# 1/rms of the query heads: four instructions of GpSimd, one per block of 128 tokens, in place of one for all four

## The chip, the cores and the metric

The kernel runs on one core of a Trainium2 chip. Five engines work on their own queues, each in order: TensorE (PE; its weight loads are listed as PEld), VectorE (DVE), ScalarE (ACT), GpSimd (POOL) and SyncE (SP), which here issues nearly all DMAs. They wait for each other through semaphores. The metric is the device time of one execution in microseconds (us), the median of several runs.

## What is computed

A transformer-like encoder layer on two sequences of 512 tokens and 1024 channels: a half-step feed-forward network, a mixing block (grouped-query attention beside an mLSTM memory), and a second half-step feed-forward network. The change touches the attention's queries. Their projection is split into 8 heads of 64, each head is divided by its root mean square, scaled by a gain, and rotated:

```
def rms_norm(x, g):
    xf = x.astype(jnp.float32)
    y = xf * lax.rsqrt(jnp.mean(xf * xf, axis=-1, keepdims=True) + EPS)
    return (y * g.astype(jnp.float32)).astype(x.dtype)
...
    h = rms_norm(x, mix_norm)
    proj = h @ w_in
...
    aq = apply_rope(rms_norm(aq.reshape(B, S, ATT_HEADS, ATT_HEAD_DIM), q_norm), cos, sin)
    ak = apply_rope(rms_norm(ak.reshape(B, S, ATT_KV_HEADS, ATT_HEAD_DIM), k_norm), cos, sin)
    av = av.reshape(B, S, ATT_KV_HEADS, ATT_HEAD_DIM)
    att = gqa_block_attention(aq, ak, av)
```

For a token there are 8 such numbers, one per head; for the 512 tokens, as 4 blocks of 128 on the partitions, a tile of 128 x 32.

## The kernel before

The program goes through the first feed-forward network for both sequences together, then the mixing of sequence 0, the mixing of sequence 1 (begun while the output projection of sequence 0 is still under way), and the second feed-forward network. Matmuls run in fp32 split into a high and a low part (three matmuls for one product), so TensorE is the engine with by far the most work.

In the mixing of a sequence, `mix` first projects keys, values and gate inputs (`kv_done`), then the queries (`q_done`), with tokens on the partitions: four PSUM banks, one per block of 128 tokens. From there:

- `q_done` works through the four blocks. ScalarE copies a block out of PSUM (L811), squares it (L758, in `sumsq`), and VectorE sums the squares of each head (L759) into 8 columns of the tile `ssq`, which has 32 columns.
- When all four blocks are summed, `rstd_cols` (L161 to L168) adds a small constant (L165) and takes the power -0.5 (L167), both on GpSimd, for all 32 columns at once.
- `q_rope(b)` rotates block `b`: `rope_apply` multiplies by the 1/rms (L770) and by the tables (L774, L779) and adds (L781), on VectorE. Then the result is split into a high and a low part (L631 on ScalarE, L632 on VectorE), TensorE transposes it, four heads at a time (L915), and ScalarE copies it to `qT` (L916). The scores of the attention (L975) read `qT`.

Between them stand, in the same stretch, the gates of the memory (L856 to L865), the turning of the keys (`k_turn`, L821 and L823), and the projections of the memory's queries and keys (L729 on TensorE, L892 on VectorE, weights through L213 and L214). A framework's scheduler fixes each engine's order at build time, by priorities; at run time every queue is in order. `small(w, tag)` gives a tile of `w` columns, two buffers for each tag; `rstd_cols` takes its result from a pool with four buffers for each width.

Of the kernel before, what the change touches and what calls it, by code (L numbers as in the profile page):

```python
# [26 lines left out]
def encoder(ctx, tc, I, outs):  # L27
# [14 lines left out]
    def nm(s):  # L42
        n_id[0] += 1
        return f"{s}_{n_id[0]}"

    @contextmanager
    def shifted(n):

        tc.cur_priority += n
        yield  # L50
        tc.cur_priority -= n
# [8 lines left out]
    def T2(dtype=F32, tag="t2"):  # L60
        if tag in ("eb", "ac"):
            i = boxes[tag]
            boxes[tag] += 1
            return boxes["tile"][:, i % 4 + (4 if tag == "ac" else 0), :]
        if tag == "R":
            return spool.tile([P, S], dtype, tag="R", bufs=2, name=nm("R"))
        n = {"t2": 11, "f2": 4}[tag]
        return tpool.tile([P, S], dtype, tag=tag, bufs=n, name=nm(tag))
# [47 lines left out]
    def PT():  # L116
        return pt.tile([P, S], F32, tag="t", name=nm("pst"))

    def f(ap):
        return ap.bitcast(F32)  # L120
# [40 lines left out]
    def rstd_cols(v, width, eps=EPS):  # L161

        a = spool.tile([P, width], F32, tag=f"rs{width}", bufs=4, name=nm("rs"))
        if eps:
            nc.gpsimd.tensor_scalar(a, v, eps, None, op0=ALU.add)  # L165
            v = a
        nc.gpsimd.tensor_tensor(a, v, nhalf[:, 0:width], op=ALU.pow)  # L167
        return a  # L168
# [460 lines left out]
    def split(src, hi, lo, eng=None):  # L629

        nc.scalar.activation(hi, src, AF.Copy)  # L631
        (eng or V_).tensor_tensor(lo, src, f(hi), op=ALU.subtract)  # L632


    HA, HK, DA = 8, 2, 64
# [3 lines left out]
    def small(w, tag):  # L639
        return spool.tile([P, w], F32, tag=tag, bufs=2 if tag != "asm" else 6, name=nm(tag))  # L640
# [4 lines left out]
    tabs = []  # L645
# [88 lines left out]
    def mix(s, xh, xl, early=None, extra=None, after=None):  # L734
# [21 lines left out]
        def sumsq(t, to):  # L756
            q2 = T2()
            nc.scalar.activation(q2, t, AF.Square, scale=DA ** -0.5)  # L758
            V_.tensor_reduce(to, q2.rearrange("p (h e) -> p h e", e=DA), axis=AX.X, op=ALU.add)  # L759

        def rope_apply(t, rq, tab, bsel):

            cg, sg = tab
            if bsel is None:
                nb, cb, sb = 4, cg.unsqueeze(2).to_broadcast([P, 4, 2, DA]), sg
            else:
                nb, cb, sb = 1, cg[:, bsel].unsqueeze(1).to_broadcast([P, 8, DA]).unsqueeze(1), sg[:, bsel:bsel + 1]
            hn_ = 8 // nb
            n = T2()
            V_.tensor_tensor(n.rearrange("p (h e) -> p h e", e=DA), t.rearrange("p (h e) -> p h e", e=DA),  # L770
                             rq.unsqueeze(2).to_broadcast([P, 8, DA]), op=ALU.mult)
            o, m = T2(), T2()
            v4 = lambda x: x.rearrange("p (b h e) -> p b h e", b=nb, e=DA)
            V_.tensor_tensor(v4(o), v4(n), cb, op=ALU.mult)  # L774
            v5 = lambda x: x.rearrange("p (b h i two) -> p b h i two", b=nb, h=hn_, two=2)
            s4 = sb.rearrange("p b (i two) -> p b i two", two=2)
            for bb in range(nb):
                for e in range(2):
                    V_.tensor_tensor(v5(m)[:, bb, :, :, e], v5(n)[:, bb, :, :, 1 - e],  # L779
                                     s4[:, bb, :, e].unsqueeze(1).to_broadcast([P, hn_, DA // 2]), op=ALU.mult)  # L780
            V_.tensor_tensor(o, o, m, op=ALU.add)  # L781
            return o
# [22 lines left out]
        qraw, rq = [], []  # L805

        def q_done(pq):
            ssq = small(32, "ssq")
            for b in range(4):
                t = T2()  # L810
                nc.scalar.activation(t, pq[b], AF.Copy, scale=r[s][:, b:b + 1])  # L811
                sumsq(t, ssq[:, b * 8:(b + 1) * 8])
                qraw.append(t)
            rq.append(rstd_cols(ssq, 32))

        def k_turn():
            for hk in range(HK):
# [87 lines left out]
            return win_cols(2320 + h * P, done)  # L905

        def q_rope(b):
            qo = rope_apply(qraw[b], rq[0][:, b * 8:(b + 1) * 8], tabs[0], b).rearrange("p (h e) -> p h e", e=DA)
            for g in range(2):
                qs = T2(F32R).rearrange("p (h u e) -> p h u e", u=2, e=DA)  # L910
                split(qo[:, g * 4:g * 4 + 4], qs[:, :, 0, :], qs[:, :, 1, :])
                with shifted(60):
                    p = PT()
                    for h in range(4):
                        nc.tensor.transpose(p[:, h * P:(h + 1) * P], f(qs[:, h]).rearrange("p u e -> p (u e)"), ident)  # L915
                    nc.scalar.activation(qT[:, g * 4:g * 4 + 4, b * P:(b + 1) * P],  # L916
                                         p.rearrange("p (h t) -> p h t", t=P), AF.Copy)

        go(*tok_proj(xh, xl, [(512, 256), (2304, 16)], 2, kv_done))
        if early:  # L920
            early()
        go(*tok_proj(xh, xl, [(0, 512)], 2, q_done), mem_qk(0, 0))
        yield None
        gates()
        k_turn()
        for b in range(4):
            q_rope(b)
# [281 lines left out]
    def turn(s, k, bank):  # L1209
        p = bank()  # L1210
        for b in range(4):
            nc.tensor.transpose(p[:, b * P:(b + 1) * P], raws[s][:, b, k * P:(k + 1) * P], ident)
        return p
# [58 lines left out]
    for k in range(HK_):  # L1272
        x1l, x1u = x1[2 * k % 4], x1[(2 * k + 1) % 4]
        for t, kk, bank, kr in ((x1l, k, PS, orow[3]), (x1u, k + HK_, PT, orow[4])):
            p = turn(1, kk, bank)
# [220 lines left out]
```

## Time and profile before

| | |
|---|---|
| median of 3 runs | 2094.67 us (2092.39 to 2095.3) |
| span of the profiled execution | 2089.2 us (from its first to its last instruction; the profile gives no time of its own beyond it) |
| PE busy | 2062.1 us, 99% |
| DVE busy | 1537.8 us, 74% |
| ACT busy | 896.4 us, 43% |
| POOL busy | 137.8 us, 7% |
| mixing of sequence 0: queries summed, 1/rms taken | 690 to 701 us |
| mixing of sequence 1: the same | 1041 to 1052 us |

How to read the rows: "L759" is line 759 of the kernel, "ssq<-t" says what is written from what, "128x8" is partitions by elements. A row of the timeline has start, duration, engine, line and operation, and in brackets how long the engine had been idle and what ended that. A row of the groups has count, busy time in us, mean ns of one instruction, and the idle time before it. A row of one line's instructions has minimum, median and maximum in ns. A row of the waits has the total in us, the number of times, and the longest. Matmuls are pipelined, so that their shown durations overlap; their rhythm is the distance of their starts.

### The profile page before, as it was taken

The page shows a single profiled execution, that of the slowest core. Times are in us where ns is not written, and L with a number is a line of the kernel's source. Part 1 is how long each engine was busy: PE and PEld are TensorE (multiplying, and loading weights), DVE is VectorE, ACT ScalarE, POOL GpSimd, SP SyncE. Part 2 cuts the span into 40 slices and gives each one's busy share as a digit, 9 for nine tenths or more (in the row PEclk, how much of TensorE's full clock was granted, in tenths as well). Part 3 has the DMA queues.
Part 4 walks back from the last instruction along what each step waited for, and adds up shares of the span by engine and source line. Part 5 has one row for each costly group of instructions (what it writes and reads, how often), then busy time and mean ns, then how long its engine had stood idle before and what let it go on. Part 6 is the DMA issues. An engine that isn't in the chain of part 4 may idle for free.

```text
span 2089.2 us, 27103 instructions
## 1 busy us (share of the span) xinstructions
PE 2062.1 (99%) x9488; PEld 1696.6 (81%) x9488; DVE 1537.8 (74%) x2612; ACT 896.4 (43%) x1645; POOL 137.8 (7%) x145
## 2 busy tenths in 40 slices
PE   8999999999999999999999999999999999999998
PEld 6888888888888777888887788888888888888887
DVE  6888988786796698574557845445888888795796
ACT  7544444442235466463444543323544444442222
POOL 1000000001004112110220000001000000000010
PEclk9999999999999999999999999999999999999999
DMA  9655655699766646778776345677656555599753
GB/s 286 198 178 185 202 171 178 207 347 355 264 221 234 194 149 209 252 241 278 224 252 211 121 152 182 204 251 244 205 169 216 184 179 182 180 342 351 273 189 116
DMA packets 304185, 458.52 MB, mean 219 GB/s; under 512 B 20304, under 2 KB 170848, under 8 KB 303024
## 3 DMA queue, kind: packets, MB, share of 16 engines
q1 hardware_dynamic: 303456, 455.52, 65.2%
q0 software_dynamic: 592, 1.27, 0.3%
q8 instruction: 75, 1.23, 0.2%
q14 instruction: 62, 0.51, 0.1%
HBM read 289.82 MB, written 166.89 MB: 219 GB/s over the span
## 4 chain that ended last, share of the span: by engine, by line
PE 93%; DVE 2%; DMA 1%; ACT 1%; issue 1%; POOL 1%; SPq 0%; DVEq 0%; POOLq 0%; ACTq 0%
PE mm L729 18%; PE pss L307 17%; PE pst L307 11%; PE mm L307 11%; PE mm L563 8%; PE pst L563 4%; PE pss L563 4%; PE mm L713 4%; PE pso L563 3%; PE pso L1002 1%; PE pso L713 1%; PE pss L975 1%; PE pst L994 1%; PE pso L1141 1%; PE pss L729 1%; PE pst L729 1%
## 5 line engine op out<-in xcount | busy, mean ns | idle before, releaser
L729 PE MATMUL mm<-xh,w 128*128 128x512 f32 x896 | 292.3, 395 | 0.4 <-DMA w<-wpark 0.4
L307 PE MATMUL pss<-xc,w 128*128 128x512 f32 x1056 | 256.4, 392 | 0.0
L307 PE MATMUL mm<-xc,w 128*128 128x512 f32 x1056 | 252.9, 391 | 3.6 <-ACT w L265 1.6
L307 PE MATMUL pst<-xc,w 128*128 128x512 f32 x1056 | 253.7, 389 | 0.0
L307 PEld LDWEIGHTS pss<-xc,w 128*128 128x128 f32 x1056 | 197.0, 188 | 47.2 <-DVE t L338 6.6
L307 PEld LDWEIGHTS mm<-xc,w 128*128 128x128 f32 x1056 | 197.5, 188 | 46.0 <-ACT w L265 2.5
L307 PEld LDWEIGHTS pst<-xc,w 128*128 128x128 f32 x1056 | 198.3, 188 | 41.2
L729 PEld LDWEIGHTS mm<-xh,w 128*128 128x128 f32 x896 | 168.3, 189 | 34.5 <-DMA w<-wpark 0.8
L563 PE MATMUL mm<-rt,w 128*128 128x512 f32 (+1 forms) x819 | 189.1, 385 | 0.0
L729 PE MATMUL mm<-xl,w 128*128 128x512 f32 x448 | 177.0, 395 | 0.0
L563 PEld LDWEIGHTS mm<-rt,w 128*128 128x128 f32 x819 | 151.7, 188 | 29.9
L265 ACT ACTIVATE w<-t 128x512 fp32r<-128x512 f32 x176 | 107.0, 627 | 138.3 <-issue 55.2
L266 DVE TENSOR_TENSOR w<-t,w 128x512 fp32r<-128x512 f32 x176 | 118.3, 689 | 53.8 <-ACT w L265 51.8
L307 PE MATMUL pss<-xc,f 128*128 128x512 f32 x528 | 126.8, 389 | 0.0
L307 PEld LDWEIGHTS pss<-xc,f 128*128 128x128 f32 x528 | 99.2, 188 | 20.5
L631 ACT ACTIVATE w<-wr 128x512 fp32r<-128x512 f32 x72 | 45.1, 632 | 137.6 <-PE pso L563 70.1
L729 PEld LDWEIGHTS mm<-xl,w 128*128 128x128 f32 x448 | 84.7, 189 | 16.6
L631 ACT ACTIVATE w<-t 128x512 fp32r<-128x512 f32 x82 | 51.8, 632 | 107.9 <-PE pst L563 62.4
L563 PE MATMUL pst<-rt,w 128*128 128x512 f32 x396 | 93.7, 389 | 0.0
L563 PE MATMUL pss<-rt,w 128*128 128x512 f32 x396 | 93.7, 389 | 0.0
L213 ACT ACTIVATE w<-wr 128x1024 fp32r<-128x1024 f32 (+1 forms) x56 | 57.4, 1028 | 76.0 <-PE mm L729 28.2
L214 DVE TENSOR_TENSOR w<-wr,w 128x1024 fp32r<-128x1024 f32 (+1 forms) x56 | 68.1, 1216 | 27.2 <-ACT w L213 26.9
(331 smaller groups left out, 3673.6 us busy)
## 6 DMA issues: line engine op xcount, KB each, us to landing
rt<-rbuf SPq DMA_DIRECT2D x154, 512.0 KB, 5.5
wpark<-w SPq DMA_DIRECT2D x104, 512.0 KB, 3.3
w<-wpark SPq DMA_DIRECT2D x104, 512.0 KB, 4.7
wr<-in_ffn_w_gate_dram SPq DMA_DIRECT2D x62, 512.0 KB, 5.5
rbuf<-tab SPq DMA_DIRECT2D x102, 256.0 KB, 4.3
wr<-in_ffn_w_up_dram SPq DMA_DIRECT2D x44, 512.0 KB, 4.7
rbuf<-f SPq DMA_DIRECT2D x72, 256.0 KB, 4.1
wr<-in_w_in_dram SPq DMA_DIRECT2D x36, 512.0 KB, 6.4
```

The lines of the kernel that those rows point to most:

```text
L213: pin(nc.scalar.activation(hi, raw, AF.Copy))
L214: pin(lo_eng.tensor_tensor(lo, raw, f(hi), op=ALU.subtract))
L265: pin(nc.scalar.activation(t[:, 0], src, AF.Copy))
L266: pin(V_.tensor_tensor(t[:, 1], src, f(t[:, 0]), op=ALU.subtract))
L307: nc.tensor.matmul(p, a[:, k, :], xt[:, b, k, :], start=(first and k == 0 and i == 0), stop=(k == HK_ - 1 and i == 2), skip_group_check=True)
L563: nc.tensor.matmul(p, u[:, a, d * P:(d + 1) * P], r[:, b, ts], start=(first and q == 0 and k == 0), stop=(q == len(us) - 1 and k == 2), sk ...
L631: nc.scalar.activation(hi, src, AF.Copy)
L713: nc.tensor.matmul(p[b][:, :N], a[:, k, bs], w_[:, kl, :], start=(k == 0 and i == 0), stop=(k == KD - 1 and i == 2))
L729: nc.tensor.matmul(p, a[:, k, :], b, start=(k == 0 and i == 0), stop=(k == n - 1 and i == 2))
L975: nc.tensor.matmul(p, qT[:, h, b * P:(b + 1) * P], kv[:, hk * 2 + j, :], start=(j == 0), stop=(j == 1))
L994: nc.tensor.transpose(p[:, b * P:(b + 1) * P], Ps[b][:, kb * P:(kb + 1) * P], ident)
L1002: nc.tensor.matmul(po, Vst[:, kv_, hk, :], w, start=(kv_ == 0 and i == 0), stop=(kv_ == 3 and i == 1))
```

## The change

The sums of each block get a tile of their own, `ssq0` to `ssq3`, 8 columns wide, and `rstd_cols` is called once per block inside the loop. `q_rope(b)` takes the result of its own block. Nothing is computed otherwise, and both sequences run the new code.

```
         def q_done(pq):
-            ssq = small(32, "ssq")
             for b in range(4):
-                t = T2()
+                t, ssq = T2(), small(8, f"ssq{b}")
                 nc.scalar.activation(t, pq[b], AF.Copy, scale=r[s][:, b:b + 1])
-                sumsq(t, ssq[:, b * 8:(b + 1) * 8])
+                sumsq(t, ssq)
                 qraw.append(t)
-            rq.append(rstd_cols(ssq, 32))
+                rq.append(rstd_cols(ssq, 8))
...
         def q_rope(b):
-            qo = rope_apply(qraw[b], rq[0][:, b * 8:(b + 1) * 8], tabs[0], b).rearrange("p (h e) -> p h e", e=DA)
+            qo = rope_apply(qraw[b], rq[b], tabs[0], b).rearrange("p (h e) -> p h e", e=DA)
```

The file is one line shorter behind this place, so that L941 of the kernel before is L940 in the changed one. On GpSimd, in the mixing of sequence 0, this stood from the keys' 1/rms (`ssk`) to the first rows of the memory (`box`):

```order
L165 TENSOR_SCALAR rs_359_5366<-ssk_357_5362 128x8
L167 TENSOR_TENSOR rs_359_5366<-rs_359_5366,nhalf_93 128x8
L165 TENSOR_SCALAR rs_388_5540<-ssq_379_5519 128x32
L167 TENSOR_TENSOR rs_388_5540<-rs_388_5540,nhalf_93 128x32
L941 TENSOR_TENSOR box_331_5195<-box_331_5195,tab_272_4143 128x512 x2
```

At the same place in the changed kernel (the powers are the L167):

```order
L165 TENSOR_SCALAR rs_359_5366<-ssk_357_5362 128x8
L167 TENSOR_TENSOR rs_359_5366<-rs_359_5366,nhalf_93 128x8
L165 TENSOR_SCALAR rs_382_5525<-ssq0_380_5520 128x8
L167 TENSOR_TENSOR rs_382_5525<-rs_382_5525,nhalf_93 128x8
L165 TENSOR_SCALAR rs_386_5534<-ssq1_384_5529 128x8
L167 TENSOR_TENSOR rs_386_5534<-rs_386_5534,nhalf_93 128x8
L165 TENSOR_SCALAR rs_390_5543<-ssq2_388_5538 128x8
L167 TENSOR_TENSOR rs_390_5543<-rs_390_5543,nhalf_93 128x8
L165 TENSOR_SCALAR rs_394_5552<-ssq3_392_5547 128x8
L167 TENSOR_TENSOR rs_394_5552<-rs_394_5552,nhalf_93 128x8
L940 TENSOR_TENSOR box_331_5195<-box_331_5195,tab_272_4143 128x512 x2
```

One pair of 32 columns has become four pairs of 8, in the same place of the queue; in sequence 1 it is the same.

On VectorE, this stood from the last block's sums to the second block's first multiplication:

```order
L759 TENSOR_REDUCE ssq_379_5519<-t2_387_5537 128x8
L865 COPY f2_398_5586<-pst_397_5581 4x512
L770 TENSOR_TENSOR t2_403_5613<-t2_380_5520,rs_388_5540 128x512
L774 TENSOR_TENSOR t2_404_5615<-t2_403_5613,tab_272_4143 128x512
L779 TENSOR_TENSOR t2_405_5616<-t2_403_5613,tab_272_4143 128x256 x2
L781 TENSOR_TENSOR t2_404_5615<-t2_404_5615,t2_405_5616 128x512
L770 TENSOR_TENSOR t2_410_5639<-t2_382_5525,rs_388_5540 128x512
```

And in the changed kernel:

```order
L759 TENSOR_REDUCE ssq3_392_5547<-t2_393_5549 128x8
L864 COPY f2_404_5598<-pst_403_5593 4x512
L770 TENSOR_TENSOR t2_409_5625<-t2_379_5519,rs_382_5525 128x512
L774 TENSOR_TENSOR t2_410_5627<-t2_409_5625,tab_272_4143 128x512
L779 TENSOR_TENSOR t2_411_5628<-t2_409_5625,tab_272_4143 128x256 x2
L781 TENSOR_TENSOR t2_410_5627<-t2_410_5627,t2_411_5628 128x512
L770 TENSOR_TENSOR t2_416_5651<-t2_383_5528,rs_386_5534 128x512
```

No instruction has moved; the two L770 read two results (`rs_382`, `rs_386`) where they read one (`rs_388`). The orders of TensorE, ScalarE and SyncE are those of before.

## Prediction

> **What bounds the kernel now.** I read the profile's page first, then the waits of TensorE, then the two places where the changed lines run, in order of time.
>
> ```profile
> PE 2062.1 (99%) x9488; PEld 1696.6 (81%) x9488; DVE 1537.8 (74%) x2612; ACT 896.4 (43%) x1645; POOL 137.8 (7%) x145
> ```
>
> TensorE is busy 99% of the span: it is the bound. Of GpSimd's 137.8 us only what TensorE waits for can move the end. The waits say where that is, TensorE's over the whole span first, then VectorE's between 690 and 800 us (who waited for whom, us in total, times, longest):
>
> ```profile
> PE pst L915 <- DVE t L632: 4.7, 2, 4.4
> DVE t L770 <- POOL rs L167: 5.4, 1, 5.4
> ```
>
> TensorE's longest wait of the whole program, 4.4 us, is for the first transposes of the rotated queries (L915), and VectorE stands 5.4 us ahead of the same chain for GpSimd's 1/rms (L167). In order of time, in the mixing of the first sequence:
>
> ```profile
> 690.32 0.69 DVE L759 TENSOR_REDUCE ssq<-t 128x8 f32<-128x512 f32 x1 [1.17 <-ACT t L758]
> 692.39 0.68 DVE L759 TENSOR_REDUCE ssq<-t 128x8 f32<-128x512 f32 x1
> 693.16 0.68 DVE L759 TENSOR_REDUCE ssq<-t 128x8 f32<-128x512 f32 x1
> 694.53 0.66 DVE L759 TENSOR_REDUCE ssq<-t 128x8 f32<-128x512 f32 x1
> 695.12 0.67 DVE L865 COPY f<-pst 4x512 f32<-4x512 f32 x1
> 695.28 0.31 POOL L165 TENSOR_SCALAR rs<-ssq 128x32 f32<-128x32 f32 x1 [21.22 <-DVE ssq L759]
> 695.67 5.46 POOL L167 TENSOR_TENSOR rs<-rs,nhalf 128x32 f32<-128x32 f32 x1
> ...
> 698.20 0.60 ACT L823 ACTIVATE kv<-pst 128x512 fp32r<-128x512 f32 x1 [0.26 <-PE pst L821]
> ...
> 700.06 0.39 PE L729 MATMUL mm<-xl,w 128*128 128x512 f32 x1
> 700.29 0.39 PE L729 MATMUL mm<-xh,w 128*128 128x512 f32 x1
> 701.16 0.69 DVE L770 TENSOR_TENSOR t<-t,rs 128x512 f32<-128x512 f32 x1 [5.37 <-POOL rs L167]
> ...
> 703.28 0.69 DVE L781 TENSOR_TENSOR t<-t,t 128x512 f32<-128x512 f32 x1
> ...
> 704.01 0.72 ACT L631 ACTIVATE t<-t 128x256 fp32r<-128x256 f32 x2 [5.21 <-DVE t L781]
> 704.50 0.75 DVE L632 TENSOR_TENSOR t<-t,t 128x256 fp32r<-128x256 f32 x2
> ...
> 705.06 1.94 PE L915 MATMUL pst<-ident,t 128*128 128x128 f32 x8 [4.38 <-DVE t L632]
> ```
>
> The first block's sums are there at 691.0 (690.32 + 0.69), yet its 1/rms comes at 701.1, with the last block's. VectorE has nothing else from 695.79 on, and TensorE's queue is in order: its last matmul begins at 700.29, and all that stands behind L915 waits until 705.06.
>
> In the second sequence the same pair hides:
>
> ```profile
> 1046.37 5.46 POOL L167 TENSOR_TENSOR rs<-rs,nhalf 128x32 f32<-128x32 f32 x1
> 1048.97 0.69 DVE L632 TENSOR_TENSOR qk<-f,qk 128x512 fp32r<-128x512 f32 x1 [0.70 <-ACT qk L631]
> 1049.92 1.23 DVE L214 TENSOR_TENSOR w<-wr,w 128x1024 fp32r<-128x1024 f32 x1 [0.26 <-ACT w L213]
> ...
> 1061.66 0.67 DVE L770 TENSOR_TENSOR t<-t,rs 128x512 f32<-128x512 f32 x1
> ```
>
> It ends at 1051.83, and L770 comes at 1061.66 without a wait: work of the output projection lies between. Whatever is gained is gained in the first sequence.
>
> **What the change costs on GpSimd.** Per sequence one addition and one power of 32 columns go, and four pairs of 8 columns come. Both sizes stand in the trace, since the keys already use 8 columns:
>
> ```profile
> L167 POOL TENSOR_TENSOR rs<-rs,nhalf 128x32 f32<-128x32 f32 x2 | 10.9, 5460 | 0.2
> L167 POOL TENSOR_TENSOR rs<-rs,nhalf 128x8 f32<-128x8 f32 x2 | 3.3, 1669 | 0.2
> L165 POOL TENSOR_SCALAR rs<-ssk 128x8 f32<-128x8 f32 x2 | 0.5, 250 | 0.5 <-DVE ssk L759 0.5
> ```
>
> A pair costs 0.25 + 0.08 between them + 1.67 = 2.00 us, and with a start 0.09 us after the sums (695.19 to 695.28) the four end so:
> - block 0: sums 691.01, pair 691.10 to 693.10
> - block 1: sums 693.07, pair 693.16 to 695.16
> - block 2: sums 693.84, pair 695.2 to 697.2
> - block 3: sums 695.19, pair 697.24 to 699.24
>
> GpSimd works 8.0 us in place of 5.8, but nothing is queued behind: its next work (L941) waits for a DMA (its row stands with the rivals). In the second sequence the four would end by 1050.4, and VectorE comes at 1061.66: cost nothing.
>
> **What is late next.** The order of VectorE, ScalarE, TensorE and SyncE is the same. VectorE is free at 695.79 and block 0 is there at 693.10, with 2.7 us to spare; L770 goes from 701.16 to 695.82, 5.34 us sooner. The rotation (L770 to L781) then ends at 698.63 instead of 703.97. ScalarE's split would start at 698.67, but its last key copy ends at 698.80, so 0.15 us are lost there. Block 0's first transposes are ready at 705.06 - 5.34 + 0.15 = 699.87. TensorE comes there after its matmul of 700.29, in its rhythm of 0.23 us (700.06 to 700.29) at 700.52. **The whole wait goes**, with 0.65 us of cover: 705.06 - 700.52 = **4.54 us**.
>
> The wait cost more than its length, as the stages by window show (the columns: length, busy time of PE, PEld, DVE, ACT and POOL, granted clock, DMA):
>
> ```profile
> 700.50:705.10 4.60, 0.22 (x2) 0.07 (x2) 3.87 (x8) 0.72 (x2) 0.62 (x1) 0.78 0.00 0
> 705.10:709.80 4.70, 4.70 (x16) 4.02 (x17) 3.99 (x8) 3.36 (x7) 0.00 (x0) 0.50 0.00 0
> ...
> 709.78 0.44 PE L729 MATMUL mm<-xl,w 128*128 128x512 f32 x1
> ...
> 712.58 1.03 PE L915 MATMUL pst<-ident,t 128*128 128x128 f32 x8
> 713.37 0.47 PE L729 MATMUL mm<-xl,w 128*128 128x512 f32 x1
> 713.68 0.63 PE L729 MATMUL mm<-xh,w 128*128 128x512 f32 x2
> ```
>
> For 4.7 us after the wait the granted clock is 0.50. There 8 transposes and 7 matmuls take 709.78 - 705.06 = 4.72 us. At full clock, by the second block's rows, 8 transposes take 0.79 (712.58 to 713.37), the next matmul 0.31 and six more 0.23 each: 2.47 us. Without the wait there is no dip: **2.25 us** more. The sum on TensorE is 4.54 + 2.25 = **6.8 us**.
>
> VectorE has gained only 5.2 at that point. Does it hold TensorE up next? TensorE wants block 1's transposes at 712.58 - 6.79 = 705.79; VectorE's split of block 1 starts at 710.27, so its first half stands at 710.65 - 5.19 = 705.5. That just fits. In the kernel before, VectorE then waits for TensorE twice, and there it makes up its arrears:
>
> ```profile
> 710.27 0.75 DVE L632 TENSOR_TENSOR t<-t,t 128x256 fp32r<-128x256 f32 x2
> 714.80 0.69 DVE L892 TENSOR_TENSOR f<-mm,R 128x512 f32<-128x512 f32 x1 [0.77 <-PE mm L729]
> 721.18 0.69 DVE L892 TENSOR_TENSOR f<-mm,R 128x512 f32<-128x512 f32 x1 [0.89 <-PE mm L729]
> ```
>
> These 1.66 us exceed the 1.6 that it lacks; from 722 on all engines stand 6.8 us earlier. The DMA engines are idle when this happens (share 0.00 from 700.5 to 709.8), so no transfer is cut short, and later transfers follow buffers that come free 6.8 us sooner as well.
>
> **Unknown: VectorE beside GpSimd.** Before, VectorE idled while this power ran; now the pairs of blocks 2 and 3 lie beside the rotation, whose operands are both in SBUF. No gain is possible from that, only a loss. Rows for both ends:
>
> ```profile
> 1061.30 2.18 POOL L158 TENSOR_TENSOR R<-R,t 128x512 f32<-128x512 f32 x1 [9.46 <-ACT t L157]
> 1062.36 1.66 DVE L774 TENSOR_TENSOR t<-t,tab 128x512 f32<-128x512 f32 x1
> L774 DVE TENSOR_TENSOR t<-t,tab x10: 684/687/1659, 675.8 to 1076.4; 128x512 f32<-128x512 f32 x10
> ```
>
> The last row gives the least, median and longest of the ten L774: 0.69 us is usual, and the one beside GpSimd's addition of 512 columns took 1.66. So the two can exclude each other. But beside the 5.46 us power at 1046.37 VectorE ran L632 in 0.69 and L214 in 1.23, both with two operands in SBUF and back to back with what ScalarE gave them: a power does not hold VectorE up, once it has read its few columns. The ends are 0 and, if each instruction of GpSimd blocked for its whole length, the 3.3 us of the first rival below. I take the nearest row, the power's own, and for the short addition of block 3 at most its 0.25; the 0.65 us of cover hold that, so 0 at the end.
>
> The Trainium skill, "SBUF — State Buffer", section "SBUF: two separate sides", says the shared port pair is an exclusive lock held for the whole instruction, also against a VectorE instruction with two SBUF inputs; by that the time would be the first rival's. The rows of 1048.97 and 1049.92 speak against it for the power; that of 1062.36 bears it out for the long addition.
>
> **Rivals.**
> 1. *The pairs block VectorE for their whole length* (or its waits join them). Then L770 starts at 697.2, and 0.25 + 1.67 more of block 3's pair fall into the rotation: 3.3 us of 5.34 are lost, the transposes stand at 703.2, TensorE waits 2.65 us. The gain is 4.54 - 2.65 = 1.9, if the dip stays whole, and 1.9 + 2.25 = 4.1 if it goes: 2090.5 to 2092.8. For it speaks the row of 1062.36, against it those of 1048.97 and 1049.92.
>    The Trainium skill, "TensorE: Matmul & The Clock Gate", Part 1, puts the drop to half clock after an idle window of about 3.4 us; by that rule a wait of 2.65 us would mostly keep the clock, and the end at 2090.5 would be the likelier one. The 4.4 us wait above agrees with it; no run here shows one of that length.
> 2. *The gain is partly taken back* in the attention, where VectorE is nearly full:
>
> ```profile
> 750.00:800.00 50.00, 48.01 (x238) 37.91 (x237) 47.16 (x90) 30.62 (x63) 10.47 (x9) 1.00 0.59 175
> L941 POOL TENSOR_TENSOR box<-box,tab 128x512 f32<-128x512 f32 x16 | 23.7, 1485 | 118.7 <-DMA box<-ebuf 114.4 <-DVE st L946 4.2
> L982 DVE TENSOR_SCALAR t<-t,asm x64: 469/479/1515, 725.6 to 1198.4; 128x512 f32<-128x512 f32 x64
> ```
>
>    There VectorE works 47.16 of 50 us, and GpSimd's L941 begins when a DMA lands. The longest of the 64 L982 took 1.52 us where the median is 0.48, a clash of 1.04 us. The shift moves VectorE against these transfers, and can add or drop such clashes. Three more cost 3.1: 2094.67 - 6.8 + 3.1 = 2091.0. Against it: the transfers follow buffers of the same engines, and shift too.
> 3. *Slower*: the same clashes, from seven more on (of 16 L941). Seven cost 7.3 us, over the 6.8: 2095.2. Nothing in the trace says that the new phase is that much worse.
> 4. *It does not do what it says*: if L770 of block 0 still came after all four powers, at 699.27, it would be 3.45 us later than in the forecast, and so would the transposes: 703.3, a wait of 2.8 us, and a gain of 1.7 to 4.0, or 2090.7 to 2093.0. Against it: each L770 reads its own tile (the order above).
>
> **How the numbers follow.** The profiled execution's span is 2089.2 us; the median of the runs is 2094.67, 5.5 more, for what lies around the span. The sum is 6.8 of the span, 2082.4, and taken from the median 2094.67 - 6.8 = **2087.9**. Chances: forecast 0.74, rivals 1 and 4 together 0.11, rival 2 0.12, slower 0.03. The range goes down by the spread of the runs (their fastest is 2.3 below the median) to 2085.5, and up to rival 2's time, 2091.0, which takes in rival 1's better end; it leaves out the rest of rival 1 and the slower case. A measurement of this kernel can tell 0.2%, 4.2 us, from no change: 2090.5. The forecast lies below that, and of rivals 1, 2 and 4 the milder cases (0.07): faster 0.81, same 0.16, slower 0.03.
>
> **What would show it.** Right: four powers of 1.67 us in a row from 691.4; L770 at 695.8 with no wait for GpSimd; L915 without a wait; granted clock 1.00 from 700 on; the second sequence's L770 still without a wait. Wrong: a power of 8 columns far above 1.7 us or L774 at over 1 us beside it (rival 1); more rows of L982 above 1 us, and TensorE's busy share from 750 to 800 falling (rivals 2 and 3).

## The result, and the profile after

| | before | changed |
|---|---|---|
| median of 6 runs | 2092.57 us (2091.05 to 2095.3) | 2086.37 us (2084.65 to 2088.08) |
| span of the profiled execution | 2089.2 us | 2085.3 us |

The ratio of the times is 0.9967, with a 95% interval of 0.9957 to 0.9977. Of 2092.57 us that is 6.9 us less (4.8 to 9.0). The means of the runs, 2093.1 and 2086.2 us, lie 6.9 us apart, their medians 6.2; here and below a gain is worked out from the ratio. The line of busy times on the page of the changed kernel:

```profile
PE 2060.8 (99%) x9488; PEld 1695.4 (81%) x9488; DVE 1537.1 (74%) x2612; ACT 895.8 (43%) x1645; POOL 143.9 (7%) x157
```

GpSimd has 6.1 us more to do and twelve more instructions, and the kernel is shorter. The place of the change in order of time, from the timeline of the changed kernel (start, duration, engine and line, with the idle time before it in brackets):

```profile
693.35 0.69 DVE L759 TENSOR_REDUCE ssq<-t 128x8 f32<-128x512 f32 x1 [1.48 <-ACT t L758]
694.12 0.24 POOL L165 TENSOR_SCALAR rs<-ssq 128x8 f32<-128x8 f32 x1 [17.05 <-DVE ssq L759]
694.45 1.67 POOL L167 TENSOR_TENSOR rs<-rs,nhalf 128x8 f32<-128x8 f32 x1
696.20 0.24 POOL L165 TENSOR_SCALAR rs<-ssq 128x8 f32<-128x8 f32 x1
696.52 1.67 POOL L167 TENSOR_TENSOR rs<-rs,nhalf 128x8 f32<-128x8 f32 x1
698.15 0.67 DVE L864 COPY f<-pst 4x512 f32<-4x512 f32 x1
698.27 1.25 POOL L165 TENSOR_SCALAR rs<-ssq 128x8 f32<-128x8 f32 x1
698.75 0.67 DVE L770 TENSOR_TENSOR t<-t,rs 128x512 f32<-128x512 f32 x1
699.45 0.69 DVE L774 TENSOR_TENSOR t<-t,tab 128x512 f32<-128x512 f32 x1
699.60 2.06 POOL L167 TENSOR_TENSOR rs<-rs,nhalf 128x8 f32<-128x8 f32 x1
700.86 0.69 DVE L781 TENSOR_TENSOR t<-t,t 128x512 f32<-128x512 f32 x1
...
702.16 0.77 DVE L632 TENSOR_TENSOR t<-t,t 128x256 fp32r<-128x256 f32 x2
...
703.54 1.03 PE L914 MATMUL pst<-ident,t 128*128 128x128 f32 x8
...
717.30 0.69 DVE L891 TENSOR_TENSOR f<-mm,R 128x512 f32<-128x512 f32 x1 [0.24 <-PE mm L729]
```

The 1/rms of block 0 is there at 696.12 (694.45 + 1.67), one pair behind its sums. L770 follows VectorE's own work at 698.75, with no idle time before it, and the transposes (L914, before L915) start without a wait. The granted clock stays at full, as the stages by window show (length, busy time of PE, PEld, DVE, ACT and POOL, granted clock, DMA):

```profile
700.50:705.10 4.60, 4.58 (x27) 3.96 (x27) 4.55 (x10) 2.59 (x6) 3.44 (x3) 1.00 0.01 4
705.10:709.80 4.70, 4.70 (x26) 4.01 (x25) 4.02 (x7) 3.61 (x7) 0.00 (x0) 1.00 0.48 192
```

In the same two windows of the kernel before, TensorE worked only 0.22 of the first 4.60 us, where it now works 4.58, and the clock was 0.78 and 0.50, where it is 1.00 in both.

**Why the spans differ by only 3.9 us.** Two profiles have to be laid on each other at a common event before times are compared. The first sums (L759) lie at 693.35 here and at 690.32 before: the changed kernel's profiled execution is 3.03 us *late* at a place that the change has not yet touched. Nothing of the change runs in the first 40 us, and the clock was lower there in this execution of the changed kernel:

```profile
0.00:40.00 40.00, 30.45 (x139) 25.06 (x140) 21.34 (x38) 26.57 (x56) 8.51 (x16) 0.89 0.90 289
```

and the same window of the kernel before:

```profile
0.00:40.00 40.00, 32.06 (x148) 26.22 (x149) 22.68 (x39) 27.38 (x57) 7.97 (x16) 1.00 0.92 295
```

The first and last starts of one line's matmuls, which run from the first network to the second, show the same; before, then changed:

```profile
L307 PE MATMUL pss<-xc,w x1056: 386/389/505, 78.7 to 1855.6; 128*128 128x512 f32 x176
```

```profile
L307 PE MATMUL pss<-xc,w x1056: 387/389/504, 81.6 to 1851.8; 128*128 128x512 f32 x176
```

At the start 2.9 us late, at the end 3.8 early. So between them lie 6.7 to 6.9 us (3.9 of the span and the 3.03 of the start), which is what the timed runs show.

### The profile page after: what moved, and what is told of

The parts are those of the page before. It is cut to its first block, busy times and chain, and to the rows that moved or that the text cites. A ratio compares the mean times of both kernels' runs of the same rounds, so it can differ in the third digit from the quotient of the medians.

```text
span 2085.3 us, 27115 instructions
## 1 busy us (share of the span) xinstructions
PE 2060.8 (99%) x9488; PEld 1695.4 (81%) x9488; DVE 1537.1 (74%) x2612; ACT 895.8 (43%) x1645; POOL 143.9 (7%) x157
## 4 chain that ended last, share of the span: by engine, by line
PE 94%; DVE 2%; DMA 1%; ACT 1%; issue 1%; POOL 0%; SPq 0%; POOLq 0%; DVEq 0%; ACTq 0%
PE mm L729 20%; PE pss L307 17%; PE pst L307 11%; PE mm L307 10%; PE mm L563 8%; PE pst L563 4%; PE pss L563 4%; PE mm L713 4%; PE pso L563 3%; PE pso L1001 1%; PE pso L713 1%; PE pss L974 1%; PE pst L993 1%; PE pso L1140 1%; PE pst L729 1%; PE pss L729 1%
```

## The experiments

The theory: all of the gain comes from the moment at which block 0's 1/rms reaches VectorE in the first sequence. TensorE's wait for L915 goes with its length, and with it the stretch at half clock behind it, which only a long wait brings. The second sequence counts for nothing, the number and width of the powers only by that moment, and a power of GpSimd does not hold VectorE up. The expectations say what it and its rivals would give. All runs are compared with the kernel before on the same chip (median 2093.05 us of 21 runs for the first four, 2092.82 us of 28 for the last four). Lines behind the edit have other numbers in these kernels: L914 of the changed kernel is L917, L921 or L925. The last column is TensorE's wait for the first transposes of the first sequence.

| run | median, us | ratio and 95% interval | TensorE's wait, us |
|---|---|---|---|
| first sequence alone | 2086.45 | 0.9967 (0.9955 to 0.9980) | none |
| second sequence alone | 2092.97 | 0.9999 (0.9990 to 1.0008) | 4.4 |
| two pairs | 2086.84 | 0.9969 (0.9956 to 0.9981) | none |
| one and three | 2088.0 | 0.9976 (0.9967 to 0.9985) | 1.7 |
| short power | 2086.95 | 0.9972 (0.9962 to 0.9983) | 0.6 |
| late, 16 columns | 2088.2 | 0.9978 (0.9969 to 0.9988) | 1.6 |
| late, 24 columns | 2089.65 | 0.9987 (0.9978 to 0.9996) | 2.8 |
| late, 32 columns | 2092.83 | 0.9998 (0.9989 to 1.0007) | 4.1 |

**Runs 1 to 4: other groups of blocks.** The loop takes the blocks in groups; a group's sums stand in one tile, and it has one pair on GpSimd (`GROUPS` stands for the groups that each run names):

```
-            for b in range(4):
-                t, ssq = T2(), small(8, f"ssq{b}")
-                nc.scalar.activation(t, pq[b], AF.Copy, scale=r[s][:, b:b + 1])
-                sumsq(t, ssq)
-                qraw.append(t)
-                rq.append(rstd_cols(ssq, 8))
+            for bs in GROUPS:
+                ssq = small(8 * len(bs), f"ssq{bs[0]}_{len(bs)}")
+                for i, b in enumerate(bs):
+                    t = T2()
+                    nc.scalar.activation(t, pq[b], AF.Copy, scale=r[s][:, b:b + 1])
+                    sumsq(t, ssq[:, i * 8:(i + 1) * 8])
+                    qraw.append(t)
+                v = rstd_cols(ssq, 8 * len(bs))
+                rq.extend(v[:, i * 8:(i + 1) * 8] for i in range(len(bs)))
```

**The first sequence alone** (groups of one in sequence 0, one group of four in sequence 1):

> Four powers of 8 columns in the first sequence alone, one of 32 in the second. Theory (the whole gain is TensorE's wait in the first sequence, 4.5 us, and the slow clock behind it, 2.3 us): as the changed kernel, 6.8 us faster than before, ratio 0.9967; no wait of L915 there. Rival (both sequences gain by the earlier powers): half, 3.4 us, ratio 0.9984.

2086.45 us, 6.9 us less than before (4.2 to 9.4): the whole gain.

**The second sequence alone** (the other way round):

> Four powers of 8 columns in the second sequence alone, one of 32 in the first. Theory: no gain, ratio 1.000 within 0.001; the first sequence still shows TensorE's wait of about 4.4 us and a granted clock of 0.50 behind it. Rival (both sequences gain): 3.4 us, ratio 0.9984.

2092.97 us, 0.2 us less (2.1 less to 1.7 more): none of it. The wait of the first sequence is there as before, in its timeline:

```profile
706.04 1.94 PE L917 MATMUL pst<-ident,t 128*128 128x128 f32 x8 [4.38 <-DVE t L632]
```

**Two pairs** (blocks 0 and 1, blocks 2 and 3, in both sequences):

> Two powers of 16 columns, one for blocks 0 and 1, one for blocks 2 and 3. By the powers of 8 and 32 columns one of 16 takes 2.93 us. Theory: block 0's 1/rms comes 0.65 us later than VectorE could use it, just what the cover holds; TensorE waits 0 to 0.2 us, 6.6 to 6.8 us faster than before, ratio 0.9968. Rival (each block must come by itself, at its own sums): 2 to 4 us of the gain are lost.

2086.84 us, a gain of 6.5 us (4.0 to 9.2). Its timeline:

```profile
693.88 2.93 POOL L167 TENSOR_TENSOR rs<-rs,nhalf 128x16 f32<-128x16 f32 x1
696.84 0.69 DVE L770 TENSOR_TENSOR t<-t,rs 128x512 f32<-128x512 f32 x1 [0.68 <-POOL rs L167]
697.73 3.31 POOL L167 TENSOR_TENSOR rs<-rs,nhalf 128x16 f32<-128x16 f32 x1
...
700.90 1.03 PE L917 MATMUL pst<-ident,t 128*128 128x128 f32 x8
```

VectorE does wait, for 0.68 us, but TensorE does not. The time alone would leave room for a loss of up to 2.8 us; it is the timeline that shows none. And the second power begins at 697.73 and runs beside the rotation, whose L770 starts before it: had it held VectorE up for its 3.31 us, L917 would stand 7.2 us behind that L770 (3.90, as in the kernel before from 701.16 to 705.06, and 3.31); it stands 4.06 us behind it.

**One and three** (block 0, then the other three):

> One power of 8 columns for block 0, then one of 24 (4.2 us) for blocks 1 to 3. Theory: VectorE's first multiplication is on time, but its second, which stands ahead of block 0's split in VectorE's order, comes 1.3 us late; TensorE waits 0.7 us, the clock stays full, 6.1 us faster than before, ratio 0.9971. Rival (block 0's power alone decides): 6.8 us, no wait of TensorE.

2088.0 us, a gain of 5.0 us (3.1 to 6.9). The direction is the theory's, but the wait is 1.7 us, not the 0.7 reckoned. In the timeline:

```profile
696.14 1.26 POOL L165 TENSOR_SCALAR rs<-ssq 128x24 f32<-128x24 f32 x1 [2.19 <-DVE ssq L759]
696.58 0.67 DVE L770 TENSOR_TENSOR t<-t,rs 128x512 f32<-128x512 f32 x1
697.48 4.55 POOL L167 TENSOR_TENSOR rs<-rs,nhalf 128x24 f32<-128x24 f32 x1
702.06 0.69 DVE L770 TENSOR_TENSOR t<-t,rs 128x512 f32<-128x512 f32 x1 [2.65 <-POOL rs L167]
...
703.23 1.06 PE L917 MATMUL pst<-ident,t 128*128 128x128 f32 x8 [1.70 <-DVE t L632]
```

Block 0 is early; block 1 is late, and its L770 stands ahead of block 0's split (L632) in VectorE's queue, so block 0's transposes wait for block 1's 1/rms. The extra 1.0 us is GpSimd's: its addition of 24 columns took 1.26 us and the power 4.55, where the same two took 0.28 and 4.20 in this run's second sequence. That is 1.3 us lost, of which 0.3 did not reach TensorE, because the cover was larger than reckoned (below). VectorE's L770 beside the addition took its usual 0.67. It is GpSimd that is held. The time's interval just takes in the rival's 6.8 us; the wait in the timeline speaks against it.

**Run 5: a short power in the kernel before.** One instruction for the sums of all four blocks, as before, but in the first sequence the power takes only block 0's 8 columns, so that this kernel leaves out the power of blocks 1 to 3:

```
-            rq.append(rstd_cols(ssq, 32))
+            if s:
+                rq.append(rstd_cols(ssq, 32))
+                return
+            a = spool.tile([P, 32], F32, tag="rs32", bufs=4, name=nm("rs"))
+            G_.tensor_scalar(a, ssq, EPS, None, op0=ALU.add)
+            G_.tensor_tensor(a[:, 0:8], a[:, 0:8], nhalf[:, 0:8], op=ALU.pow)
+            rq.append(a)
```

> The kernel before with one addition of 32 columns, and in the first sequence a power of only the first 8 columns behind it: blocks 1 to 3 of that sequence lack their power, so that part of the computation is left out. Theory (TensorE's wait decides, not the splitting into blocks): block 0's 1/rms comes at 697.4 on the clock of before instead of 701.1, TensorE waits 0.8 us, the clock stays full, 6.0 us faster than before, ratio 0.9971. Rival (the gain comes from starting at each block's own sums): at most half the gain, ratio 0.9984 or above.

2086.95 us, a gain of 5.9 us (3.6 to 8.0):

```profile
695.94 1.67 POOL L819 TENSOR_TENSOR rs<-rs,nhalf 128x8 f32<-128x8 f32 x1
697.64 0.69 DVE L770 TENSOR_TENSOR t<-t,rs 128x512 f32<-128x512 f32 x1 [1.58 <-POOL rs L819]
...
701.54 1.06 PE L921 MATMUL pst<-ident,t 128*128 128x128 f32 x8 [0.60 <-DVE t L632]
```

With no sums taken earlier and no pair added, the shorter power alone brings nearly all of the gain. It is the time until the 1/rms is there that counts, not how many instructions there are. Since the other blocks have no power of their own here, their columns are ready at the same moment as block 0's; the run does not part block 0 from them.

**Runs 6 to 8: block 0 late again, by a chosen amount.** In the changed kernel, block 0's pair goes behind block 1's, and its power is taken over `n` copies of its 8 columns (n = 2, 3, 4, a power of 16, 24 or 32 columns; each run has the numbers in place of `n` and `8 * n`), of which the first is used. The work of VectorE, ScalarE and TensorE is that of the changed kernel:

```
                 sumsq(t, ssq)
                 qraw.append(t)
+                if s == 0 and b == 0:
+                    ssq0 = ssq
+                    continue
                 rq.append(rstd_cols(ssq, 8))
+                if s == 0 and b == 1:
+                    a = spool.tile([P, 8], F32, tag="rs8", bufs=4, name=nm("rs"))
+                    G_.tensor_scalar(a, ssq0, EPS, None, op0=ALU.add)
+                    wide = small(8 * n, "wide")
+                    G_.tensor_tensor(wide.rearrange("p (n e) -> p n e", e=8), a.unsqueeze(1).to_broadcast([P, n, 8]),
+                                     nhalf[:, 0:8].unsqueeze(1).to_broadcast([P, n, 8]), op=ALU.pow)
+                    rq.insert(0, wide[:, 0:8])
```

**16 columns:**

> The changed kernel with block 0's pair behind block 1's on GpSimd in the first sequence, and block 0's power taken over its 8 columns twice (16 columns, 2.9 us). TensorE waits 1.9 us for block 0. Theory (the slow clock is a step that a short wait does not bring): granted clock stays 1.00, 4.9 us faster than before, ratio 0.9977. Rival (the slow clock costs in proportion to the wait, 0.5 us for 1 us): 4.0 us faster, ratio 0.9981.

2088.2 us, a gain of 4.6 us (2.5 to 6.5). The rows of the timeline and, with the same columns as above, of a window:

```profile
700.28 0.69 DVE L770 TENSOR_TENSOR t<-t,wide 128x512 f32<-128x512 f32 x1 [2.58 <-POOL wide L822]
...
704.18 1.06 PE L925 MATMUL pst<-ident,t 128*128 128x128 f32 x8 [1.59 <-DVE t L632]
```

```profile
704.00:709.00 5.00, 4.82 (x26) 4.14 (x27) 4.64 (x9) 3.80 (x7) 1.56 (x1) 1.00 0.06 23
```

Here a wait of 1.59 us leaves the clock at 1.00: 8 transposes and 7 matmuls take 2.53 us (704.18 to 706.71). And 6.9 - 1.6 = 5.3 lies in the interval. The time alone doesn't exclude a loss of more than the wait; the clock row does for this execution.

**24 columns:**

> As e6 with 24 columns (4.2 us): TensorE waits 3.1 us. Theory: if 3.1 us is below the step, the clock stays 1.00 and it is 3.7 us faster than before, ratio 0.9982; if above, the clock falls to 0.50 for some 4 us and it is 1.4 us faster, ratio 0.9993. Rival (in proportion): 2.1 us faster, ratio 0.9990, with a dip of 3 us.

2089.65 us, a gain of 2.7 us (0.8 to 4.6). Its timeline and its windows:

```profile
700.18 0.69 DVE L770 TENSOR_TENSOR t<-t,wide 128x512 f32<-128x512 f32 x1 [3.84 <-POOL wide L822]
...
704.08 1.37 PE L925 MATMUL pst<-ident,t 128*128 128x128 f32 x8 [2.83 <-DVE t L632]
...
708.19 0.39 PE L729 MATMUL mm<-xl,w 128*128 128x512 f32 x1
```

```profile
704.00:705.00 1.00, 0.92 (x7) 0.95 (x8) 1.00 (x3) 0.25 (x1) 1.00 (x1) 0.85 0.00 0
705.00:706.00 1.00, 1.00 (x5) 0.90 (x4) 1.00 (x3) 0.86 (x2) 0.46 (x1) 0.50 0.07 16
...
708.00:709.00 1.00, 1.00 (x6) 0.82 (x5) 1.00 (x2) 1.00 (x3) 0.00 (x0) 0.94 0.40 160
```

In this execution the clock fell to 0.50 within the first microsecond after the wait and was back before 709: 8 transposes and 7 matmuls took 4.11 us (704.08 to 708.19), where 2.47 are taken at full clock, so the stretch cost 1.64 us. Wait and stretch make 6.9 - 2.8 - 1.6 = 2.4 us of gain. But this execution took 2092.43 us, near the top of its eleven runs (2087.16 to 2093.1). A part of that has nothing to do with block 0: in the second sequence TensorE waited twice for weights, and the clock fell to 0.50 once more:

```profile
1099.01 0.47 PE L729 MATMUL mm<-xh,w 128*128 128x512 f32 x1 [1.09 <-DMA w<-wpark]
1100.16 0.83 PE L729 MATMUL mm<-xh,w 128*128 128x512 f32 x2 [0.46 <-DMA w<-wpark]
```

```profile
1100.00:1101.00 1.00, 0.84 (x3) 0.69 (x4) 0.10 (x1) 0.00 (x0) 0.00 (x0) 0.82 1.17 318
1101.00:1102.00 1.00, 1.00 (x3) 0.79 (x3) 0.00 (x0) 0.00 (x0) 0.00 (x0) 0.50 0.86 219
```

In the changed kernel's profile the clock stays at 1.00 there. As for block 0, the gain of 2.7 us lies between 6.9 - 2.8 = 4.1 and 2.4 with an interval that holds both. Whether every run has the stretch at half clock was not seen: inconclusive.

**32 columns:**

> As e6 with 32 columns (5.5 us): four powers by block as in the changed kernel, but block 0's 1/rms arrives when it did before, TensorE waits 4.4 us. Theory: the wait and the dip to 0.50 come back and the gain is gone, ratio 1.000. Rival (some of the gain is from the other blocks' earlier 1/rms): 1 to 3 us remain, ratio 0.9986 to 0.9995.

2092.83 us, 0.4 us less than before (2.3 less to 1.5 more). Its timeline and one of its windows:

```profile
700.67 0.69 DVE L770 TENSOR_TENSOR t<-t,wide 128x512 f32<-128x512 f32 x1 [5.10 <-POOL wide L822]
...
704.57 1.94 PE L925 MATMUL pst<-ident,t 128*128 128x128 f32 x8 [4.12 <-DVE t L632]
...
709.29 0.63 PE L729 MATMUL mm<-xl,w 128*128 128x512 f32 x1
```

```profile
708.00:709.00 1.00, 1.00 (x4) 0.79 (x3) 0.75 (x2) 1.00 (x3) 0.00 (x0) 0.50 0.00 0
```

The wait is back, the same 15 instructions take 4.72 us as in the kernel before, the clock is 0.50, and the gain is gone, although every block still has a pair of its own. Of the others only block 1's 1/rms is early in this run; those of blocks 2 and 3 stand at 703.61 and 705.95, later than in the kernel before (701.13). That they count for nothing is seen from the waits: in no profile of these kernels does L770 of block 2 or 3 wait for GpSimd.

No variant was faster than the changed kernel; the one that changes only the first sequence is as fast.

## Why the prediction was right

**The wait goes, with its length.** Predicted 4.54 us. With the 3.03 us by which the two profiles are apart, L915 of the kernel before would stand at 708.09; L914 stands at 703.54, 4.55 us earlier. The prediction's arrival of TensorE, 700.52, becomes 703.55. The first sequence alone brings the whole gain, the second alone none, and with block 0 late again by 32 columns nothing is left of it. The run with one and three adds that block 1 has to be there soon after, since its L770 stands ahead of block 0's split. L770 of block 0 starts while block 2's pair is still running, so it does not wait for all four (rival 4 is out).

**The half clock goes too.** Predicted 2.25 us. The next memory projection's L892 would stand at 721.18 + 3.03 = 724.21, and L891 starts at 717.30: 6.91 us earlier, of which 4.55 are the wait. The remaining 2.36 are the clock, but for 0.1: the 8 transposes and 7 matmuls from L914 on take 2.48 us (703.54 to 706.02) in place of 4.72, which is 2.24. VectorE waits for TensorE both times, for 0.89 us before and 0.24 now: VectorE has made up its arrears there, as reckoned. The sum was 6.8, the runs show 6.9 (4.8 to 9.0). An interval of 2 us either way cannot confirm it to a tenth; the two traces do.

**The first two pairs cost what their rows said, the others more.** 1.67 us for each of the first two powers, and 2.07 from pair to pair (694.45 to 696.52) where 2.00 was reckoned. The prediction's sign, four powers of 1.67 us in a row, did not come: block 2's took 2.06 us and block 3's 1.77, and the last ended at 704.10 where 702.27 was reckoned (699.24 and the 3.03). Nobody waited for it. In the second sequence the last power ends at 1046.99, and L770 comes long after it, without a wait:

```profile
1045.32 1.67 POOL L167 TENSOR_TENSOR rs<-rs,nhalf 128x8 f32<-128x8 f32 x1
1058.17 0.67 DVE L770 TENSOR_TENSOR t<-t,rs 128x512 f32<-128x512 f32 x1
```

**VectorE is not held (rival 1 is out).** From the start of L770 to the end of L781 it took 2.80 us (698.75 to 701.55) with GpSimd's pair beside it, and 2.81 (701.16 to 703.97) with GpSimd idle. But the clash that the prediction looked for exists, with the other engine as the loser: block 2's addition took 1.25 us instead of 0.24 and its power 2.06 instead of 1.67. The prediction allowed up to 0.25 us of VectorE's time; it was nothing there, and 1.4 us of GpSimd's at block 2, which here nobody waits for. In the run with one and three it was waited for, and cost 1.0 us of the gain. For rival 1's wait of 2.65 us the prediction held the full clock likelier; the nearest run, with a wait of 2.83 us, lost it in its one profile.

The Trainium skill, "SBUF — State Buffer", section "SBUF: two separate sides", has whichever of the two engines starts first hold the shared ports for its whole instruction, while the other is blocked. The trace doesn't agree for the power: L781 started 1.26 us into a power that lasted until 701.66, and took its usual 0.69 us; it was the power that grew. Whether that is because the power has read its few columns by then, as the prediction has it, is not shown.

**The cover was a little larger.** Predicted 0.65 us between the transposes' readiness and TensorE's arrival. L915 started 0.56 us after L632 in the kernel before (704.50 to 705.06), so block 0 is ready at 702.72 here and TensorE comes at 703.54: 0.82. L770 started 0.10 earlier than reckoned, and from L770 to L632 it took 3.41 us (698.75 to 702.16) against 3.34 in the kernel before (701.16 to 704.50), so that ScalarE's key copy cost at most 0.07, not 0.15. The runs agree with one another: L770's lateness less TensorE's wait, both from the brackets, is 0.98 us with the short power (1.58 and 0.60), 0.99 with 16 late columns, 1.01 with 24, 0.98 with 32, and 0.99 in the kernel before (5.37 and 4.38). The brackets count from the end of the last matmul, 0.16 us behind the arrival by starts, so these are the same 0.82. That is also why the 0.68 us of the two pairs cost TensorE nothing, and why the waits of the three late runs were each 0.3 us shorter than expected (1.59, 2.83 and 4.12 us for 1.9, 3.1 and 4.4).

**Nothing is taken back (rivals 2 and 3 are out).** The window from 750 to 800 us and the group of rival 2, in the changed kernel:

```profile
750.00:800.00 50.00, 47.73 (x237) 37.61 (x236) 47.22 (x87) 29.50 (x60) 12.12 (x9) 1.00 0.55 180
```

```profile
L981 DVE TENSOR_SCALAR t<-t,asm x64: 469/478/1508, 721.7 to 1194.6; 128x512 f32<-128x512 f32 x64
```

TensorE works 47.73 of 50 us where it worked 48.01, in a window that by now holds work of 3.9 us later in the program; the longest clash is still 1.51 us. That the 0.28 us are no loss shows at the end: 6.91 us at L891, and 6.9 in the last row.

**What was mis-sized is the base.** The prediction took 5.5 us from the profiled span to the median to be "what lies around the span". The profiled execution of the changed kernel took 2087.08 us with a span of 2085.3: 1.8 us lie around it. The other 3.7 were the difference of two executions. The same goes for the median itself: with six runs it is 2092.57, 2.1 us lower than with three. Less 6.8 that would have been 2085.8; 2086.37 was measured. The predicted 2087.9 is 1.5 us over the measurement because of this start, and not because of a step.

## What to carry to other kernels

A small operation that serves several consumers is worth splitting by the order in which they come, if the first of them is in the queue of the engine that is the bound; what counts is when the first part is there, and here the second soon after it, while splitting what is used late brings nothing. A wait of TensorE's has two prices, its length and, where it is long, the half clock behind it, so that here the 2.5 us from a wait of 1.6 to one of 4.1 cost 4.2 (a gain of 4.6 became one of 0.4, each within some 2 us). Lay two traces on each other at an event ahead of the change before subtracting their spans: here 3 of 7 us would have been missed.

## What the runs showed of the hardware

- The wait and the clock: waits of 1.59 and 1.70 us left the granted clock at 1.00; one of 2.83 us was followed by half clock for some 3.4 us in its one profile; after those of 4.12 and 4.38 us the next 15 instructions took 4.72 us, which is 2.25 more than at full clock. In the kernel before the clock fell within the wait, 2.4 us after the last matmul had ended at 700.68:

```profile
703.00:704.00 1.00, 0.00 (x0) 0.00 (x0) 0.97 (x3) 0.00 (x0) 0.00 (x0) 0.52 0.00 0
709.00:710.00 1.00, 1.00 (x4) 0.81 (x3) 0.88 (x1) 1.00 (x4) 0.00 (x0) 0.57 0.07 29
```

If the clock is only ever 1.00 or 0.50 inside a window, these rows and the 0.50 between them give a stretch at half clock from 703.04 to 709.86, 6.8 us; by the same working it is 6.8 us with 32 columns, and 3.4 us each time in the profile with 24. These lengths are estimates, and why they are one and two times the same length is not shown. The Trainium skill, "TensorE: Matmul & The Clock Gate", Part 1, puts the drop to half clock after an idle window of about 3.4 us. The waits of 1.6 us that kept the clock agree with that; the drop 2.4 us after the last matmul, and the wait of 2.83 us, show that less can bring it. Nor does one wait's length decide alone: in the profile with 24 columns, waits of 1.09 and 0.46 us with two matmuls between them were followed by half clock as well.
- GpSimd's power takes time by columns with a fixed part: 1.67 us for 8 columns, 2.93 for 16, 4.17 to 4.20 for 24 and 5.46 for 32, about 0.4 us and 0.158 us for each column.
- When VectorE has instructions with two SBUF operands back to back, a small instruction of GpSimd among them can wait longer than one of them lasts: 0.24 us became 1.25, and 0.28 became 1.26, each until just after the end of the L770 that had started after it (699.52 and 697.40, where L770 ended at 699.42 and 697.25). By the recorded starts the instruction that started first was here the one that waited; why is not shown. The copy that VectorE had begun just before (L864) is not enough: beside the same copy (L865 there) the addition of 32 columns took 0.31 us in the kernel before, as in its second sequence.
